# Overlapping pipelines for the chunks of a delta rule, an output projection by tiles, and a last product and norm in pieces

## The chip, the core and the metric

The kernel runs on one core of a Trainium2 chip. The metric is the time of one execution on the device, in microseconds (us). The engines of the core work side by side, each through its own list of instructions in a fixed order, and wait for each other through semaphores: TensorE (PE) multiplies matrices into PSUM, of which the kernel uses eight banks of 128 x 512 float32; VectorE (DVE), ScalarE (ACT) and GpSimd (POOL) work on tiles; SyncE (SP) issues most transfers. Weight loads of PE have a column of their own (PEld). Times come from executions of the whole program; the profile and the trace come from one profiled execution.

## The reference

A transformer-like layer of width 1024 on 1024 tokens: a feed-forward block, a mixer and a second feed-forward block, each with a residual and a norm ahead, and a last norm.

```python
h = h + 0.5 * swiglu_ffn(rmsnorm(h, ffn1_norm), ffn1_w_in, ffn1_w_out)
u = rmsnorm(h, mix_norm) @ w_mix_in
cb, cc, ch, gq, gk, gv, gz, gb, ga = split(u)
y_conv = short_conv_mixer(cb, cc, ch, conv_short_w, conv_out_norm)
y_gdn = gated_deltanet_mixer(gq, gk, gv, gz, gb, ga, ...)
h = h + concatenate([y_conv, y_gdn]) @ w_mix_out
h = h + 0.5 * swiglu_ffn(rmsnorm(h, ffn2_norm), ffn2_w_in, ffn2_w_out)
return rmsnorm(h, final_norm)
```

The delta rule has 4 heads of 128 and goes over the tokens in chunks. The part that matters here is, for each chunk (decay from the running sum g of the gates):

```python
lower = strict(k_beta @ k.T * decay)
u, w = solve_unit_lower(lower, [v_beta, k_beta * exp(g)])
attn = causal(q @ k.T * decay)
v_new = u - w @ state
o = (q * exp(g)) @ state + attn @ v_new
state = state * exp(g_last) + (k * exp(g_last - g)).T @ v_new
```

The kernel takes chunks of 128 tokens, so there are eight.

## The kernel before

Activations lie with channels on partitions and tokens along the free axis, in two halves of 512 tokens. Every wide product is done in split float32: each operand is cut into a rounded part hi and a rest lo (`split`, L102 on ACT and L103 on DVE), and `mm3` issues three matmuls of 128 x 128 by 512, hi by hi, lo by hi and hi by lo (L191 to L193). Such a group is called a triple here. `mm3` ends in `tick()`, which counts triples; `later(n, f)` has f emitted n triples on.

The stages: products of the first feed-forward block (0 to about 686 us), the norm and the q, k, v projection (to about 838), the delta rule with the z and convolution projections (to 1151), the output projection (to 1241 and, in its last part, beyond), the second feed-forward block (to 1939) and the last norm.

Within the feed-forward blocks and the output projection, work comes as a list of tasks with three parts: loads, preparation (sums of weights on POOL, splits on ACT and DVE) and the run of triples. `run_tasks` emits a task's loads up to nine tasks and its preparation up to four tasks ahead of its run. `ffn_out` does its product as seven block products of eleven steps each (L539 on); each step has four triples, one for each of four banks, and an `add` behind a product adds the four banks into the residual (L554). After the fifth product half 0 of the residual is complete; its norm runs beside products six and seven: squares on ACT (L209), their sum on POOL or DVE (L211), `after(n, m)`, which has the sum over channels taken by PE (L225) n triples later and the factor spread by PE (L243) m triples after that.

In the delta-rule stage PE has two sources of work. The z and convolution units (`rest`, 16 units of 16 triples = 256) are independent of the chunks and cover them: `pump(n)` emits n triples of them. The chunk work comes from generators, a `yield` between steps:
- `build(c)`, five steps, one chunk: loads q, k, v; transposes k, q, v on PE (`flip`, L868); the decay matrix `dec` and `eb` from products with a mask (L950, L974) and exponentials on ACT; `kd` (L954, on DVE, read from the PSUM bank of the k transpose); K times K (L862) into `lt`, Q times K into `at`; all results go to DRAM.
- `solve(g)`, 33 steps: inverts the 32 x 32 diagonal blocks of four chunks on DVE (L1030, L1034).
- `finish(c)` and `scan(c)`: load a chunk's results, complete the inverse on PE, and carry the state from chunk to chunk; the chunk's output `ot` is scaled on ACT (L1149), flipped and written.
- `late_convs`: the convolutions of the second half of q, k, v (L774), one in two steps.

`drive` runs one main generator step, then `pump`, then some steps of a side generator. Chunk follows chunk: builds 0 to 3 with the late convolutions beside them, builds 4 to 7 with `solve(0)`, inverse and scan of chunks 0 to 3 with `solve(1)`; those of chunks 4 to 7 run between tasks of the output projection (`mix_out`). Small products use four PSUM banks in turn (tag `aux`), wide ones the four others (`mm`); a bank is free for the next product when its last reader is done. A scheduler behind the program may move instructions within what the dependences allow; from then on each engine's order is fixed.

## Time and profile before

| what | value |
|---|---|
| time, median of 3 runs | 1960.46 us (1956.25 to 1960.53) |
| profiled execution, time | 1959.77 us |
| profiled execution, span from first to last instruction | 1958.0 us |
| mean clock granted to PE | 0.971 |
| instructions | 25016 |
| DMA | 312.45 MB, mean 160 GB/s |

How to read it: the span is shorter than the time by what lies before the first and behind the last instruction. An engine's share of busy time is a mean over all stages; the stages are seen in the row of 40 equal slices, in which each digit is the busy share in tenths (PEclk: the granted clock in tenths):

```profile
PE   5799999999999899987799989998999999999996
DVE  4876666567865797776974356688666566677655
PEclk9899999999999999998999979998999999999998
```

A slice is 49 us. The dip in the row of PE at slices 18 and 19 (from 0) is the beginning of the delta-rule stage; the last slice holds the last norm.

### The profile page before, as it was taken

The numbers are of one execution on the slowest core, as the hardware profiler recorded it, in microseconds if no ns is written. First come the engines' busy times: TensorE is split into PE (matmuls) and PEld (weight loads), VectorE is DVE, ScalarE is ACT, GpSimd is POOL, SyncE is SP. The second block draws the span as 40 slices with busy tenths as digits, with TensorE's granted clock in tenths as the row PEclk, the third lists the DMA queues.
The fourth block names the chain that finished last, engine by engine and source line by source line (L and its number), as shares of the span: only waits on it lengthen the run. The fifth ranks groups of instructions, "written<-read, shape, count | busy, mean of one in ns | idle before, by whom it ended". The sixth has DMA issues, their size and how long they took to land.

```text
span 1958.0 us, 25016 instructions
## 1 busy us (share of the span) xinstructions
PE 1833.8 (94%) x8512; PEld 1493.6 (76%) x8512; DVE 1338.5 (68%) x1991; ACT 750.0 (38%) x1517; POOL 733.3 (37%) x510
## 2 busy tenths in 40 slices
PE   5799999999999899987799989998999999999996
PEld 4578888888888777676678877776888888888884
DVE  4876666567865797776974356688666566677655
ACT  6422323223544453377332243452323222344433
POOL 1464455355331434145311001036454355435142
PEclk9899999999999999998999979998999999999998
DMA  7144343437883423477742176423343434487532
GB/s 281 33 161 128 118 140 127 140 108 257 311 270 113 140 97 102 141 245 252 222 135 80 61 263 183 164 92 102 127 139 127 140 109 160 150 292 274 193 108 97
DMA packets 194512, 312.45 MB, mean 160 GB/s; under 512 B 27856, under 2 KB 48336, under 8 KB 194384
## 3 DMA queue, kind: packets, MB, share of 16 engines
q1 hardware_dynamic: 191216, 305.28, 47.0%
q10 hardware_dynamic: 3168, 5.57, 0.9%
q8 instruction: 67, 1.10, 0.2%
q14 instruction: 61, 0.50, 0.1%
HBM read 228.44 MB, written 82.33 MB: 159 GB/s over the span
## 4 chain that ended last, share of the span: by engine, by line
PE 74%; DVE 13%; issue 4%; DMA 3%; POOL 3%; ACT 3%; SPq 0%; POOLq 0%; DVEq 0%; ACTq 0%
PE ps_ps L192 20%; PE ps_ps L191 20%; PE ps_ps L193 20%; PE ps_mm L191 3%; PE ps_mm L192 3%; PE ps_mm L193 3%; DVE wlo L103 3%; PE ps_aux L862 1%; DVE lo L103 1%; DVE xb L1034 1%; DVE sv L1030 1%; DVE cv L774 1%; POOL T L110 1%; DMA raw<-w_in 1%; DVE h L301 1%
## 5 line engine op out<-in xcount | busy, mean ns | idle before, releaser
L191 PE MATMUL ps_ps<-hi,whi 128*128 128x512 f32 x1400 | 554.1, 396 | 23.0 <-DVE c L389 11.4
L193 PE MATMUL ps_ps<-hi,wlo 128*128 128x512 f32 x1400 | 552.7, 395 | 13.0 <-DVE wlo L103 12.9
L192 PE MATMUL ps_ps<-lo,whi 128*128 128x512 f32 x1400 | 553.0, 395 | 5.3 <-DVE lo L103 5.2
L103 DVE TENSOR_TENSOR wlo<-raw,whi 128x512 fp32r<-128x512 f32 x280 | 267.3, 964 | 119.4 <-ACT whi L102 118.4
L103 DVE TENSOR_TENSOR wlo<-T,whi 128x512 fp32r<-128x512 f32 x244 | 235.3, 978 | 144.5 <-ACT whi L102 142.4
L191 PEld LDWEIGHTS ps_ps<-hi,whi 128*128 128x128 f32 x1400 | 266.8, 191 | 85.4 <-issue 12.3
L193 PEld LDWEIGHTS ps_ps<-hi,wlo 128*128 128x128 f32 x1400 | 267.3, 191 | 71.7 <-DVE wlo L103 16.0
L192 PEld LDWEIGHTS ps_ps<-lo,whi 128*128 128x128 f32 x1400 | 266.9, 191 | 63.1 <-DVE lo L103 8.0
L110 POOL TENSOR_TENSOR T<-raw 128x512 f32<-128x512 f32 x144 | 224.6, 1561 | 232.3 <-DMA raw<-w_out 91.5
L191 PE MATMUL ps_ps<-ghi,whi 128*128 128x512 f32 x616 | 241.8, 393 | 7.2 <-ACT whi L102 7.2
L192 PE MATMUL ps_ps<-glo,whi 128*128 128x512 f32 x616 | 241.9, 393 | 1.4 <-DVE glo L103 1.4
L193 PE MATMUL ps_ps<-ghi,wlo 128*128 128x512 f32 x616 | 241.7, 393 | 1.2 <-DVE wlo L103 1.2
L102 ACT CAST whi<-raw 128x512 fp32r<-128x512 f32 x280 | 170.2, 617 | 86.1 <-PE ps_mm L192 19.1
L102 ACT CAST whi<-T 128x512 fp32r<-128x512 f32 x244 | 146.4, 617 | 81.4 <-POOL T L110 44.8
L191 PE MATMUL ps_mm<-hi,whi 128*128 128x512 f32 x384 | 158.0, 412 | 0.9 <-DVE u L400 0.9
L192 PE MATMUL ps_mm<-lo,whi 128*128 128x512 f32 x384 | 155.2, 404 | 1.2 <-DVE lo L103 1.2
L193 PE MATMUL ps_mm<-hi,wlo 128*128 128x512 f32 x384 | 154.2, 402 | 1.4 <-DVE wlo L103 1.4
L103 DVE TENSOR_TENSOR glo<-raw,ghi 128x512 fp32r<-128x512 f32 x154 | 128.9, 838 | 38.8 <-ACT ghi L102 37.2
L191 PEld LDWEIGHTS ps_ps<-ghi,whi 128*128 128x128 f32 x616 | 116.3, 189 | 33.6 <-ACT whi L102 8.4
L193 PEld LDWEIGHTS ps_ps<-ghi,wlo 128*128 128x128 f32 x616 | 116.3, 189 | 28.0 <-DVE wlo L103 2.7
L192 PEld LDWEIGHTS ps_ps<-glo,whi 128*128 128x128 f32 x616 | 116.4, 189 | 27.3 <-DVE glo L103 2.1
L110 POOL TENSOR_TENSOR T<-raw,T 128x512 f32<-128x512 f32 x50 | 73.3, 1465 | 167.2 <-DMA raw<-w_in 129.3
(226 smaller groups left out, 2286.5 us busy)
## 6 DMA issues: line engine op xcount, KB each, us to landing
raw<-w_in SPq DMA_DIRECT2D x264, 256.0 KB, 4.6
raw<-w_out SPq DMA_DIRECT2D x154, 256.0 KB, 4.3
raw<-w_qkv SPq DMA_DIRECT2D x36, 256.0 KB, 3.4
f1S<-S SPq DMA_DIRECT2D x33, 256.0 KB, 5.0
raw<-f1A SPq DMA_DIRECT2D x33, 256.0 KB, 3.9
raw<-f1S SPq DMA_DIRECT2D x33, 256.0 KB, 3.7
f2S<-S SPq DMA_DIRECT2D x33, 256.0 KB, 5.0
raw<-f2A SPq DMA_DIRECT2D x33, 256.0 KB, 4.5
```

Source lines behind the costliest of these rows:

```text
L102: tc.keep_in_program_order(nc.scalar.copy(out=hi, in_=src))
L103: nc.vector.tensor_tensor(out=lo, in0=src, in1=hi.bitcast(F32), op=ALU.subtract)
L110: tc.keep_in_program_order(nc.gpsimd.tensor_tensor(out=out, in0=in0, in1=in1, op=op))
L191: nc.tensor.matmul(out=ps, lhsT=whi, rhs=xhi, start=start, stop=False, skip_group_check=True)
L192: nc.tensor.matmul(out=ps, lhsT=whi, rhs=xlo, start=False, stop=False, skip_group_check=True)
L193: nc.tensor.matmul(out=ps, lhsT=wlo, rhs=xhi, start=False, stop=stop, skip_group_check=True)
L301: nc.vector.tensor_tensor(out=s2, in0=s2, in1=s1, op=ALU.subtract)
L774: nc.vector.scalar_tensor_tensor(out=acc, in0=u[:, i:i + HALF], scalar=vcol(wc + i), in1=acc, op0=ALU.mult, op1=ALU.add)
L862: nc.tensor.matmul(out=ps[:, sl], lhsT=lhs[:, sl], rhs=rhs[:, sl], start=start, stop=stop)
L1030: nc.vector.tensor_tensor(out=tv, in0=lrow[:, lo:hi].unsqueeze(2).broadcast_to([nb, n, j + 1]), in1=xrow[:, 0:j + 1].unsqueeze(1).broadcas ...
L1034: nc.vector.tensor_tensor(out=xv, in0=xv, in1=tv, op=ALU.subtract)
```

## The change

1. `pipeline(gens, lag)` steps several generators in turn; the next one starts when the last one has gone `lag` steps. Builds 0 to 5 go through it with lag 3 (the late convolutions and then `solve(0)` beside them), builds 6 and 7 and then `solve(1)` become the side work of the inverses and scans of chunks 0 to 3, which go through it with lag 5; those of chunks 4 to 7 too, beside the output projection.
2. In `build`, a step boundary is put behind the first loads, and the mask product for `eb` stands ahead of `kd`. In `scan`, a step boundary is put ahead of the flip of `ot`.
3. One set of 22 tiles (`gd`) serves the builds and then the scans, cut in two ways by `rings`, so that several builds have tiles of their own.
4. `PACE`, the triples of cover per step, goes from 2.5 and 4.5 to 3.0 and 2.6.
5. `mix_out` has a task for each of eight output tiles instead of four tasks of two tiles.
6. The norm beside products six and seven starts 14 triples after the fifth instead of 26 (first block) and 30 (second block).
7. In the second block, the last four steps of product seven are done tile by tile, each tile's add right behind it.
8. The last norm is done in two halves of columns, with 16 output transfers instead of 8 for half 1, and ACT applies its share of the gain ahead of the spread.

```diff
-PACE = (2.5, 4.5)
+PACE = (3.0, 2.6)
...
+            def one(d, stop):
+                x, w = ops["x"], ops["w"]
+                ds = slice(d * P, (d + 1) * P)
+                mm3(banks[d], w[0][:, ds], w[1][:, ds], x[0], x[1], start and k == 0, stop)
+
+            if held is None:
+                task(run, ready, loads)
+            else:
+                held.append(one)
+                task(None, ready, loads)
...
-            task(add)
+            if not by_tile:
+                task(add)
+                return
+            for d in range(KH):
+                task(lambda d=d: [one(d, i == KH - 1) for i, one in enumerate(held)] and add([d]))
...
-            nm[0].after(26, 4)
+            nm[0].after(14, 4)
...
+        gd_tiles = [slot(F32, "gd") for _ in range(22)]
+        ring, used = {"r0": [slot(F32R, "r0") for _ in range(2)]}, {}
+
+        def rings(**counts):
+            n = 0
+            for name, b in counts.items():
+                ring[name] = gd_tiles[n:n + b]
+                n += b
...
                 r0.append(r)
+            yield
...
             pd = psum("aux")
...
+            pe = psum("aux")
+            for i, r in enumerate(r0):
+                nc.tensor.matmul(out=pe, lhsT=mask[:, P:2 * P], rhs=r, start=(i == 0), stop=(i == 1))
             dec = gt_tile("dec")
             nc.scalar.activation(out=dec, in_=pd, func=AF.Exp)
+            eb = gt_tile("eb")
+            nc.scalar.activation(out=eb, in_=pe, func=AF.Exp)
...
             yield
+            yield
             pyt = flip(ot)
...
+        def pipeline(gens, lag):
+
+            gens, live = list(gens), []
+            while gens or live:
+                if gens and (not live or live[-1][1] >= lag):
+                    live.append([gens.pop(0), 0])
+                for e in list(live):
+                    if next(e[0], live) is live:
+                        live.remove(e)
+                    else:
+                        e[1] += 1
+                        yield
...
+        def second_half():
+            for _ in pipeline([build(c) for c in (6, 7)], 6):
+                pump(PACE[1])
+                yield
+            solving = solve(1)
+            for _ in solving:
+                next(solving, None)
+                yield
+
+        rings(qT=3, kT=3, vT=3, v=2, dec=3, kd=2, lt=2, eb=2)
+        drive(pipeline([build(c) for c in range(CPH)], 3), PACE[0], late, 1)
...
+        drive(pipeline([build(c) for c in (4, 5)], 3), PACE[0], side, 3)
...
+        side = second_half()
+        drive(pipeline([inverse_and_scan(c) for c in range(CPH)], 5), PACE[1], side, 1)
...
             for u in range(4):
-                task(lambda u=u: run(u), lambda u=u: ready(u), lambda u=u: loads(u))
+                task(lambda u=u: run(u, 0), lambda u=u: ready(u), lambda u=u: loads(u))
+                task(lambda u=u: run(u, 1))
...
         def between():
-            for _ in range(4):
+            for _ in range(2):
                 next(scans, None)
...
-            last[0].after(30, 4)
+            last[0].after(14, 4)
...
+        for i in range(2):
+            for b in range(2 * i, 2 * i + 2):
+                nc.tensor.matmul(out=last[1].rb[:, b * P:(b + 1) * P], lhsT=rs[:, b:b + 1].broadcast_to([P, P]),
+                                 rhs=ident, start=True, stop=True)
+            scale_out(1, slice(2 * i * P, (2 * i + 2) * P))
```

The change moves instructions on every engine. At three places the built order of before and of the change stand here.

PE, from the k flip of build 2 to that of build 3 and K times K, before. `kT`, `qT` and `vT` are a chunk's k, q and v; `ps_aux` and `ps_mm` with a number are the uses of the small and the wide banks; L974 is the mask product for `eb`, L950 that for `dec`:

```order
L862 MATMUL ps_aux_7815<-kT_7305 128x128 x4
L974 MATMUL ps_aux_7849<-r0_7314,mask_7331 128x512
L974 MATMUL ps_aux_7849<-r0_7315,mask_7331 128x512
L862 MATMUL ps_aux_7854<-qT_7303,kT_7305 128x128 x4
L868 MATMUL ps_aux_7871<-cs_68,qT_7303 128x128 x4
L868 MATMUL ps_aux_7913<-cs_68,vT_7307 128x128 x4
L868 MATMUL ps_aux_7934<-cs_68,kT_7306 128x128 x4
L950 MATMUL ps_aux_7950<-r0_7314,mask_7331 128x512
L950 MATMUL ps_aux_7950<-r0_7315,mask_7331 128x512
L862 MATMUL ps_aux_7968<-kT_7306 128x128 x4
```

The change on PE, a k flip (of `gd_7307`) and what follows it; L968 and L971 are now the mask products for `dec` and `eb`, L885 the flip, and `gd_7309` is a v tile of another chunk:

```order
L885 MATMUL ps_aux_7595<-cs_68,gd_7307 128x128 x4
L968 MATMUL ps_aux_7611<-r0_7325,mask_7331 128x512
L968 MATMUL ps_aux_7611<-r0_7326,mask_7331 128x512
L971 MATMUL ps_aux_7614<-r0_7325,mask_7331 128x512
L971 MATMUL ps_aux_7614<-r0_7326,mask_7331 128x512
L885 MATMUL ps_aux_7633<-cs_68,gd_7309 128x128 x4
L191 MATMUL ps_mm_7580<-hi_5611,whi_7411 128x512
L192 MATMUL ps_mm_7580<-lo_5612,whi_7411 128x512
L193 MATMUL ps_mm_7580<-hi_5611,wlo_7412 128x512
L191 MATMUL ps_mm_7580<-hi_5616,whi_7411 128x512
```

Before, the steps of two builds stand one behind the other, with no wide matmul between them. Now a step of a build is followed by wide matmuls; after the last row shown come ten more of them, and then K times K of `gd_7307`, so fourteen wide ones lie between this chunk's flip and its K times K.

SP, where the output projection starts, before. `y_dr001` is the second piece of the convolution's output for half 0 of the tokens, `y_dr011` that for half 1; the loads of `raw` from `y_dr000` and `y_dr001` are the first operands of the projection, and L1046 and L1049 load results of a chunk:

```order
L1184 DMA y_dr001_7262<-acc_9936 128x512
L1049 DMA xc_10761<-diag_x1_7397 128x4x32
L1155 DMA y_dr100_7265<-zt_7325 256x1x128
L1155 DMA y_dr101_7266<-zt_7325 256x1x128
L1046 DMA lts_7324<-st_lt5_7381 128x512
L1184 DMA y_dr011_7264<-acc_10009 128x512
L95 DMA raw_10249<-y_dr000_7261 128x512
L95 DMA raw_10251<-y_dr000_7261 128x512
L95 DMA raw_10253<-y_dr001_7262 128x512
```

The change at the same place, where L1064 and L1067 are the loads of a chunk and L1203 the write of the convolution's output:

```order
L1153 DMA gd_7323<-z_dr1_7260 128x4x128
L1067 DMA xc_10620<-diag_x1_7397 128x4x32
L1064 DMA gd_7322<-st_lt5_7381 128x512
L1203 DMA y_dr001_7262<-acc_9987 128x512
L95 DMA raw_10240<-y_dr000_7261 128x512
L95 DMA raw_10242<-y_dr000_7261 128x512
L95 DMA raw_10244<-y_dr001_7262 128x512
L95 DMA raw_10246<-y_dr001_7262 128x512
```

The first loads of the projection stood behind the write of `y_dr011`; they now stand directly behind that of `y_dr001`, and the write of `y_dr011` follows seventeen places later.

DVE at the end of the program, before. L554 adds a bank into the residual `h`, L211 sums the squares into `nacc`, L217 makes the mean, L1387 scales an output tile:

```order
L554 SCALAR_TENSOR_TENSOR h_15741<-ps_ps_17075,h_15741 128x512
L211 TENSOR_TENSOR nacc_17043<-nacc_17043,sq_17268 128x512
L554 SCALAR_TENSOR_TENSOR h_15771<-ps_ps_17076,h_15771 128x512
L211 TENSOR_TENSOR nacc_17043<-nacc_17043,sq_17272 128x512
L211 TENSOR_TENSOR nacc_17043<-nacc_17043,sq_17276 128x512
L211 TENSOR_TENSOR nacc_17043<-nacc_17043,sq_17280 128x512
L217 TENSOR_SCALAR ms_17288<-ps_ps_17283 128x4
L1387 SCALAR_TENSOR_TENSOR h_15677<-h_15677,vs_66,ps_ps_17292 128x512
```

The change at the same place, where L563 adds, L1456 makes the mean of two of the four token blocks, and L1430 scales half of an output tile:

```order
L563 SCALAR_TENSOR_TENSOR h_15741<-ps_ps_17077,h_15741 128x512
L211 TENSOR_TENSOR nacc_17043<-nacc_17043,sq_17267 128x512
L563 SCALAR_TENSOR_TENSOR h_15771<-ps_ps_17078,h_15771 128x512
L211 TENSOR_TENSOR nacc_17043<-nacc_17043,sq_17283 128x512
L1456 TENSOR_SCALAR last_ms_17288<-ps_ps_17287 128x2 x2
L1430 SCALAR_TENSOR_TENSOR h_15677<-h_15677,vs_66,ps_ps_17286 128x256
L1430 SCALAR_TENSOR_TENSOR h_15741<-h_15741,vs_66,ps_ps_17286 128x256
```

The sums of squares no longer stand in a row behind the adds: each follows its own add, and the ten scalings of half tiles take the place of five of whole tiles.

More of the change, by code (lines that the diff above doesn't have):

```diff
@@ L493, in early_heads, with ffn_out @@
             task(*p.head2())
-    def ffn_out(acc, fill, g_dr, w_out, t1_done, t2_done):
+    def ffn_out(acc, fill, g_dr, w_out, t1_done, t2_done, by_tile=False):
         tsum = {}
@@ L503, in get, with step @@
             return load(w_out[2 * k + row][:, c * HALF:(c + 1) * HALF])
-        def step(banks, a, b, k, start):
+        def step(banks, a, b, k, start, held=None):
             r, ops = {}, {}
@@ L537, in run, with product @@
                 for d in range(KH):
-                    ds = slice(d * P, (d + 1) * P)
-                    mm3(banks[d], w[0][:, ds], w[1][:, ds], x[0], x[1], start and k == 0, k == NK - 1)
-            task(run, ready, loads)
-        def product(banks, a, b, start, *to, then=None, after=None):
+                    one(d, k == NK - 1)
+            def one(d, stop):
[7 more added lines that the diff above has]
+                task(None, ready, loads)
+        def product(banks, a, b, start, *to, then=None, after=None, by_tile=False):
+            held = []
             for k in range(NK):
-                step(banks, a, b, k, start)
+                step(banks, a, b, k, start, held if by_tile and k >= NK - KH else None)
                 if KH <= k < KT:
@@ L548, in product, with add @@
                         task(lambda tile_=tile_: fill(*tile_))
-            def add():
-                for d in range(KH):
+            def add(ds=range(KH)):
+                for d in ds:
                     for n in to:
@@ L970, in build @@
             yield
-            pe = psum("aux")
-            for i, r in enumerate(r0):
-                nc.tensor.matmul(out=pe, lhsT=mask[:, P:2 * P], rhs=r, start=(i == 0), stop=(i == 1))
-            eb = gt_tile("eb")
-            nc.scalar.activation(out=eb, in_=pe, func=AF.Exp)
-            nc.vector.tensor_copy(out=cols(per_chunk["gl"], c), in_=heads(eb)[:, :, C - 1])
             pq = psum("aux")
@@ L1276, in drive @@
                     next(side, None)
-        def inverse_and_scan(c):
-            yield from finish(c)
-            yield from scan(c)
-        for c in range(CPH):
-            drive(build(c), late, PACE[0], 2)
+        def second_half():
[8 more added lines that the diff above has]
+        drive(pipeline([build(c) for c in range(CPH)], 3), PACE[0], late, 1)
         for _ in late:
@@ L1286, in tile_hybrid @@
         side = solve(0)
[L1287 to L1288 removed]
+        drive(pipeline([build(c) for c in (4, 5)], 3), PACE[0], side, 3)
         for _ in side:
             pass
[L1291 to L1293 removed]
+        rings(qT=2, kT=1, vT=1, v=1, dec=1, kd=1, lt=1, eb=1, kg=2, qg=2, vs=2, kds=2, at=2, lts=1, zt=1, ot=1)
+        side = second_half()
+        drive(pipeline([inverse_and_scan(c) for c in range(CPH)], 5), PACE[1], side, 1)
         for _ in side:
@@ L1393, in out_t1, with out_t2 @@
                 last[0].square(d)
-            last[0].after(30, 4)
-            last[0].then(lambda: scale_out(0))
-        ffn_out(acc, fill, g_dr, w2_out, out_t1, lambda d: last[1].square(d, nc.vector))
-        run_tasks()
-        last[1].reduce()
-        last[1].spread()
-        scale_out(1)
+            last[0].after(14, 4)
+            last[0].then(lambda: [gain(0, d) for d in range(KT) if pre_scaled(d)] and scale_out(0))
+        def out_t2(d):
+            last[1].square(d, nc.vector)
+            if pre_scaled(d):
+                gain(1, d)
+        ffn_out(acc, fill, g_dr, w2_out, out_t1, out_t2, by_tile=True)
+        run_tasks()
+        last[1].rb = psum()
+        sums = psum()
+        ms, rs = (const.tile([P, 4], F32, name=n) for n in ("last_ms", "last_rs"))
+        for i in range(2):
+            two = slice(2 * i, 2 * i + 2)
+            for b in range(2 * i, 2 * i + 2):
+                nc.tensor.matmul(out=sums[:, b:b + 1], lhsT=last[1].acc[:, b * P:(b + 1) * P], rhs=ones[:, 0:1],
+                                 start=True, stop=True)
+            nc.vector.tensor_scalar(out=ms[:, two], in0=sums[:, two], scalar1=1.0 / D, scalar2=EPS,
+                                    op0=ALU.mult, op1=ALU.add)
+            nc.gpsimd.tensor_tensor(out=rs[:, two], in0=ms[:, two], in1=pneg[:, two], op=ALU.pow)
+        for i in range(2):
+            for b in range(2 * i, 2 * i + 2):
+                nc.tensor.matmul(out=last[1].rb[:, b * P:(b + 1) * P], lhsT=rs[:, b:b + 1].broadcast_to([P, P]),
+                                 rhs=ident, start=True, stop=True)
+            scale_out(1, slice(2 * i * P, (2 * i + 2) * P))
         while queue:
```

79 lines of the change are left out of this document (36 added, 43 removed).

## The prediction

> **What bounds the kernel now.** I read the page first: busy time by engine, and the chain of work that ended last.
>
> ```profile
> PE 1833.8 (94%) x8512; PEld 1493.6 (76%) x8512; DVE 1338.5 (68%) x1991; ACT 750.0 (38%) x1517; POOL 733.3 (37%) x510
> PE 74%; DVE 13%; issue 4%; DMA 3%; POOL 3%; ACT 3%; SPq 0%; POOLq 0%; DVEq 0%; ACTq 0%
> ```
>
> TensorE (PE) is busy 94% of the span and is 74% of the chain. The change takes no matrix product away, so it can only win time in which PE stands still or runs at a low clock. The next view cuts the stages that the change rewrites into windows. Columns: window, length, then busy us and instructions of PE, weight loads, VectorE (DVE), ScalarE (ACT) and GpSimd (POOL), the clock granted to PE, the DMA share, GB/s.
>
> ```profile
> core 0: us, PE busy (x) PEld busy (x) DVE busy (x) ACT busy (x) POOL busy (x), PEclk, DMA share, GB/s
> 838.00:907.00 69.00, 54.91 (x258) 44.46 (x257) 48.72 (x92) 54.36 (x132) 31.05 (x24) 0.85 0.80 262
> 907.00:988.00 81.00, 66.52 (x340) 54.74 (x338) 62.85 (x182) 34.39 (x114) 30.17 (x25) 0.94 0.69 213
> 988.00:1123.00 135.00, 132.91 (x844) 108.12 (x844) 72.76 (x201) 38.23 (x103) 12.83 (x9) 1.00 0.30 91
> 1123.00:1151.00 28.00, 21.80 (x157) 19.42 (x156) 12.52 (x30) 10.32 (x30) 2.60 (x2) 0.70 0.56 180
> 1151.00:1241.00 90.00, 84.75 (x546) 67.47 (x545) 52.96 (x106) 34.42 (x93) 14.39 (x12) 0.94 0.65 209
> 890.00:900.00 10.00, 6.40 (x21) 4.82 (x22) 8.15 (x16) 9.80 (x25) 5.91 (x4) 0.50 0.78 267
> ...
> 1440.00:1480.00 40.00, 40.00 (x178) 33.12 (x178) 26.01 (x32) 10.90 (x20) 18.14 (x12) 1.00 0.37 126
> ```
>
> The windows are: builds 0 to 3 (838 to 907), builds 4 to 7 (907 to 988), the first four scans with the second solve (988 to 1123), the passage to the output projection (1123 to 1151), and that projection with the last scans (1151 to 1241). The last row is a stage with no gap, for comparison: 40.00 / 178 = 0.225 us for one wide matmul.
>
> What each window loses, I count as idle time plus (1 - clock) times busy time. Builds 0 to 3: 69 - 54.91 = 14.1, and 0.15 x 54.91 = 8.2, so 22.3 us. Builds 4 to 7: 14.5 + 0.06 x 66.52 = 18.5. First scans: 2.1. Passage: 6.2 + 0.30 x 21.80 = 12.7. Projection: 5.3 + 0.06 x 84.75 = 10.3. That is **66 us** in 403; more than these cannot come from this part of the program. Each fast stretch needs its neighbours to be fast, as the row of 890 to 900 shows: PE is busy 6.4 of 10 us, and runs at half clock besides.
>
> **The change part by part.**
>
> *Builds.* A build turns one chunk's q, k, v into what the scans need. The groups of PE show where it stands still; after the second bar is the idle time before a group, and what ended it.
>
> ```profile
> L868 PE MATMUL ps_aux<-cs,ot 128*128 128x128 f32 x32 | 9.8, 357 | 6.8 <-ACT ot L1149 6.8
> ...
> L868 PE MATMUL ps_aux<-cs,vT 128*128 128x128 f32 x32 | 5.9, 314 | 11.4 <-DVE kd L954 6.6 <-ACT eb L976 2.7 <-issue 2.1
> ...
> L868 PE MATMUL ps_aux<-cs,kT 128*128 128x128 f32 x32 | 5.7, 305 | 8.9 <-DVE cv L774 4.3 <-DMA kT<-qkv_dr 2.3 <-DVE xb L1034 1.4
> L868 PE MATMUL ps_aux<-cs,qT 128*128 128x128 f32 x32 | 5.4, 294 | 2.0 <-DVE bk L945 1.9
> ```
>
> Of the 28.6 us idle in the two build windows, 22.3 stand before the three flips (transposes) of the builds. The v flip waits 11.4 in all, mostly for kd: the four auxiliary PSUM banks go round, and the v flip takes the bank that kd is read from. In the order of before, sixteen small matmuls and no wide one lie between the two flips at the place shown. In the new order, steps of two builds alternate with wide triples, so these 11.4 and the q flip's 1.9 are what I expect to go: **13.3**.
>
> A wait takes their place. In the new order, the mask product for eb is issued earlier, so the K-times-K product now takes kd's bank. How long kd takes today, from the k flip on PE to kd on DVE:
>
> ```profile
> 914.67 0.63 PE L868 MATMUL ps_aux<-cs,kT 128*128 128x128 f32 x4 [0.66 <-ACT whi L102]
> ```
> ```profile
> 921.67 0.67 DVE L954 TENSOR_TENSOR kd<-ps_aux,dec 128x512 f32<-128x512 f32 x1
> ```
>
> That is 922.34 - 914.67 = 7.7 us to kd's end. Between the k flip and the K-times-K product the new order has fourteen wide matmuls in the place shown (14 x 0.225 = 3.1 us), the flip itself and another (0.6 each) and four mask products, together about 5 us. Today's 7.7 includes work of DVE that stood before kd only because two late convolution or three solve steps ran per build step. Bounds for the new wait: 0, and 8 builds x (7.7 - 5) = 22. I take 1 us each, **8**, since the squares and the exponential of the same chain are all that remains. Queued behind K-times-K on PE are the triples themselves, so all of it is lost time.
>
> The k flip's 8.9 is for DVE (4.3 for cv, a late convolution; 1.4 for the solve) and for its load (2.3). The late convolutions run one step per build step instead of two, though more steps overlap; their work is the same. I take half of cv and load as gone, **3.3**. Clock: 8.2 + 4.0 = 12.2 us are lost to it; with the gaps about halved I take half, **6.1**. Builds: 13.3 - 8 + 3.3 + 6.1 = 14.7, rounded to **14.5** (bounds: 13.3 - 22 = -8.7, and all of 40.8).
>
> The Trainium skill, "TensorE: Matmul & The Clock Gate", Part 1 (The HAM clock gate), says that the clock is either half or full, that half follows an idle window of about 3.4 us, and that a busy window of that length brings full back. The 0.50 of 890 to 900 agrees with the half; no row here shows the window's length. By this rule gaps that all fall under that length would bring back all 12.2 us and the sum would be 6 us lower.
>
> *First scans.* Two builds and the second solve move into this window, and two scans overlap. It loses 2.1 us now, so it can hardly gain; cover per step falls from 4.5 triples to 2.6, but there are more steps. I take **0** (bounds: +2, and a loss as dense as that of builds 4 to 7, 2 builds x 18.5 / 4 = 9). The same 256 triples of z and convolution are spread, none added.
>
> *Passage and output projection.* SyncE's (SP's) queue, in order:
>
> ```profile
> 1129.95 0.32 SPq L1184 DMA_DIRECT2D y_dr<-acc  x1
> ...
> 1139.76 0.35 SPq L1184 DMA_DIRECT2D y_dr<-acc  x1
> 1140.15 2.12 SPq L95 DMA_DIRECT2D raw<-y_dr  x4
> 1142.37 8.80 SPq L95 DMA_DIRECT2D raw<-w_mo  x8
> ```
>
> The projection starts with half 0 of the convolution output, the last quarter of which is written at 1129.95. Its loads stand behind the write of half 1 (1139.76) and go at 1140.15: 10.2 us later, with PE at a clock of 0.70. In the new order these loads stand right behind the half-0 write, ahead of the half-1 write. I take the 10.2 us as saved up to what the window loses, 12.7: **10** (bounds 0, if the eight weight loads of 8.80 us set the start, and 12.7). A second term: in the projection the scans' flip of ot waits 6.8 us for ACT; the extra step before it and the second scan beside it put wide triples there. I take all, **6.8** (bounds 0 and 10.3). Together **17**.
>
> *Norm in the first feed-forward output.* Waits of PE between 640 and 700, and POOL's queue there:
>
> ```profile
> PE ps_ps L191 <- ACT whi L102: 3.1, 2, 2.2
> ...
> PE ps_ps L193 <- DVE wlo L103: 1.2, 2, 0.8
> ```
> ```profile
> 660.19 4.06 POOL L211 TENSOR_TENSOR nacc<-nacc,sq 128x512 f32<-128x512 f32 x3 [16.01 <-ACT sq L209]
> 664.21 4.64 POOL L110 TENSOR_TENSOR nT<-nT,raw 128x512 f32<-128x512 f32 x3
> ```
>
> PE loses 4.3 us as product 7's weights stand on POOL behind the sums of squares, which come late since DVE did the norm's multiplications right before. With the norm 12 triples (12 x 0.675 = 8 us) earlier, that work meets product 6 instead, whose operands are prepared four tasks ahead. I take **4** (bounds 0, as preparations for product 6 now fall behind the norm, and 5).
>
> *Norm and last product in the second feed-forward output.*
>
> ```profile
> PE ps_ps L191 <- ACT whi L102: 4.1, 1, 4.1
> ...
> PE ps_ps L192 <- DVE glo L103: 0.6, 1, 0.6
> ```
> ```profile
> 1903.12 3.70 SPq L1389 DMA_DIRECT2D out_dram<-h  x6
> ```
> ```profile
> 1912.66 4.47 POOL L110 TENSOR_TENSOR nT<-nT,raw 128x512 f32<-128x512 f32 x3 [4.89 <-DMA raw<-w_out]
> ```
>
> Six output writes stand in SP's queue ahead of the last weights, POOL waits 4.89 us for these, and PE then 4.7. In the new order the norm comes 16 triples (11 us) earlier, and the writes stand three steps further from the end. Against it: the last four steps of the last product are now taken tile by tile, so its first tile needs the operands of the last step 3 steps (9 triples beyond the first tile's own three, 6 us) sooner. I take **4.5** (bounds 0 and 4.7 plus 1.7 for the clock).
>
> *Tail.*
>
> ```profile
> 1938.94 0.39 PE L193 MATMUL ps_ps<-ghi,wlo 128*128 128x512 f32 x1
> ...
> 1942.83 1.87 PE L225 MATMUL ps_ps<-cs,nacc 128*128 128x1 f32 x8 [3.49 <-DVE nacc L211]
> ...
> 1948.78 3.38 DVE L1387 SCALAR_TENSOR_TENSOR h<-h,vs,ps_ps 128x512 f32<-128x512 f32 x5 [3.88 <-ACT rbs L1380]
> ...
> 1950.12 3.98 ACTq L1389 DMA_DIRECT2D out_dram<-h  x4
> ```
>
> By tile, only one add, square and sum follow the last matmul instead of DVE's heap: of 3.49 us I take 1.2 as saved. The norm in two halves saves little: in the built order the second half's spread on PE waits for DVE's last multiplication of the first half, as both lie in one PSUM tile, and ScalarE's copy stands behind its output issues, so the pieces come one after the other. The last output issues on ACT (1950.12 to 1954.10) are fewer and smaller: about 1.3. Sum **2.5** (bounds 0, as twice the instructions may cost twice the fixed time, and 4).
>
> The Trainium skill, "PSUM — Partial Sum Buffer", section "PSUM bank collisions raise a hardware error", says that two engines must be kept from one bank at the same time, whatever the columns. The row of 1948.78 agrees in part: DVE reads the spread only after ACT's copy of it. By this rule no order of these pieces in one bank overlaps; with two banks the sum would have about 2 us more.
>
> **Sum.** 14.5 + 0 + 17 + 4 + 4.5 + 2.5 = 42.5 us. The profiled execution took 1959.77 (span 1958.0 and 1.8 around it), 0.7 under the median of 1960.46; 1959.77 - 42.5 = 1917.3, so **1917**.
>
> **Rivals.**
>
> *The other engines bind in the builds.* DVE is busy 48.72 + 62.85 of 150 us there and ACT 54.36 of the first 69; 9.80 of 10 in the row of 890. Late convolutions, solve steps and builds are the same work on them. For it: between 838 and 907 ACT leaves just 14.6 us. Against it: over both windows ACT has 88.75 of 150. Then builds gain nothing, and the first scans with two builds lose up to 9: 1917 + 14.5 = 1932, up to 1941. 25%.
>
> *Nearly everything goes.* Pipelines hide the new wait too and the clock stays full: 66 - 31.5 = 34 more, less what an edge between stages must cost, say a quarter of 66: about 1900, at the very best 1883. 13%.
>
> *Slower: the bank ring of builds.* With two builds live and four auxiliary banks, every product of a build, not K-times-K alone, waits for a reader of the other build, PE being in order. If three of the five steps wait the 2.7 us (7.7 - 5), this is 8 x 3 x 2.7 = 65 instead of the 8 I took: 1917 + 57 = 1974. It decides from (42.5 + 6) / 8 = 6 us per build over my value. For it: the wait on kd is in the built order. Against it: the other readers (exponential, lt, at) are single operations of 0.6 to 1.4 us. 6%.
>
> *The change doesn't do it:* loads of the projection stay bound by the eight weight loads and the norms by DVE. Then 17 and 8.5 fall away: 1942. 8%.
>
> **How the numbers follow.** My forecast (1905 to 1926) has 44%, the others as given; the remaining 4% are mixtures near no change. What a measurement here can tell from no change is 0.3%, 5.9 us (1954 to 1966). Faster: 44 + 25 + 13 + 8 = 90%, less 2 for the tails of the last two: 88%. Within 0.3%: 5%. Slower: 7%. The range 1890 to 1946 takes in the first rival's upper end, the fourth rival and most of the best case; outside are the slower rival, no change and the best of the best, 17%.
>
> **What would show it.** Right: PE's clock at 0.95 or more in the build stage; the wait of the v flip for kd gone; loads of y directly behind the half-0 write and the first output product some 18 us after the last convolution triple or sooner; no wait of 4 us for weights in the last product; the time from the last wide matmul to the end 2 to 3 us shorter than 1958.0 - 1939.3 = 18.7. Wrong: DVE or ACT busy over 95% of the builds; K-times-K waiting over 3 us per build; a new gap where builds 6 and 7 lie among the first scans.

## The result and the profile after

The changed kernel took 1905.0 us (median of 4 runs, 1902.51 to 1906.43), the kernel before 1958.36 beside it (4 runs, 1952.78 to 1960.53). The ratio is 0.9726 (95% interval 0.9703 to 0.9749), so it is faster by 2.7%. The profiled execution took 1906.43, its span is 1904.4: 53.6 us shorter than the span before. The forecast was 1917 with 1890 to 1946.

The page of the changed kernel, busy time by engine:

```profile
PE 1816.6 (95%) x8512; PEld 1483.8 (78%) x8512; DVE 1337.0 (70%) x1997; ACT 747.3 (39%) x1518; POOL 732.2 (38%) x514
```

PE has the same 8512 matmuls; every engine does the same work in a shorter span. Windows of the changed kernel follow (columns as before); the first three rows are builds 0 to 3, builds 4 and 5 with the rest of the first solve, and the scans with builds 6, 7 and the second solve. Then come the passage to the output projection, and the projection.

```profile
830.00:899.00 69.00, 62.97 (x316) 50.19 (x315) 53.15 (x94) 55.95 (x137) 32.15 (x25) 0.98 0.82 269
899.00:958.00 59.00, 51.47 (x243) 42.78 (x243) 46.32 (x132) 20.99 (x63) 19.25 (x15) 0.88 0.74 234
958.00:1100.00 142.00, 140.20 (x930) 115.73 (x930) 90.44 (x261) 50.84 (x163) 23.83 (x19) 1.00 0.40 124
1100.00:1118.00 18.00, 16.32 (x151) 14.68 (x148) 9.37 (x22) 5.94 (x15) 1.63 (x1) 0.62 0.69 207
1118.00:1198.00 80.00, 78.55 (x511) 65.52 (x512) 51.78 (x103) 33.55 (x94) 14.25 (x12) 1.00 0.65 218
```

Counted as in the prediction, the losses are 6.0 + 1.3 = 7.3, 7.5 + 6.2 = 13.7, 1.8, 1.7 + 6.2 = 7.9 and 1.5 us: 32 in place of 66. Builds lose 21 instead of 40.8, although two of them now lie in the scans, which lose no more than before; the passage 7.9 instead of 12.7; the projection 1.5 instead of 10.3.

Where in the program the 53.6 us came from is read on PE: the start of the n-th triple in both traces, and the difference (from the 1461st on the order of the triples is alike again).

```
triple    before     after   ahead by
 851       628.7     628.7      0.0     before product 7 of the first block
 951       708.0     702.0      6.0
1101       835.3     827.3      8.0     first builds
1461      1268.6    1228.7     39.9     second feed-forward block begins
1651      1417.4    1374.0     43.4
2351      1897.8    1854.4     43.4     last product
2400      1938.5    1888.3     50.2     last triple
end       1958.0    1904.4     53.6
```

At product 7, with the norm beside it, the change gains 6.0 us, from the first builds to the second block 31.9, in the last product 6.8 and in the tail 3.4. The 2.0 us between triples 951 and 1101 and the 3.5 between 1461 and 1651 are not credited to the change: the kernels below that have it, with the early norm, take 125.3 to 127.6 and 143.5 to 148.1 us there, the kernel before 127.3 and 148.8. The triples between 1651 and 2351, which the change leaves alone, take the same time to 0.1 us.

The flips of the builds and of `ot`, which had 29.1 us of idle time ahead of them in four rows, are one row now (L885), with K times K and its like in L879, and no wait for `kd`:

```profile
L879 PE MATMUL ps_aux<-gd 128*128 128x128 f32 x184 | 26.9, 293 | 1.8 <-ACT gd L973 0.8 <-DVE gd L1021 0.8
L885 PE MATMUL ps_aux<-cs,gd 128*128 128x128 f32 x128 | 21.1, 284 | 8.4 <-DMA gd<-qkv_dr 4.1 <-ACT junk L1008 1.7 <-DVE gd L999 1.1
```

SP's queue at the passage: the loads now stand right behind the half-0 write, as the order showed, but the first output product starts at 1118.69, 13.6 us after them (11.1 before).

```profile
1104.40 0.32 SPq L1203 DMA_DIRECT2D y_dr<-acc  x1
1105.07 2.22 SPq L95 DMA_DIRECT2D raw<-y_dr  x4
1107.34 8.70 SPq L95 DMA_DIRECT2D raw<-w_mo  x8
```

Tail:

```profile
1891.31 0.61 PE L1454 MATMUL ps_ps<-cs,nacc 128*128 128x1 f32 x4 [2.17 <-DVE nacc L211]
...
1896.82 1.19 PE L1461 MATMUL ps_ps<-cs,last_rs 128*128 128x128 f32 x4 [2.63 <-POOL h L1428]
...
1898.49 2.09 POOL L1428 TENSOR_TENSOR h<-h,rbs 128x256 f32<-128x256 f32 x3 [1.74 <-ACT rbs L1424]
1899.25 1.70 ACTq L1432 DMA_DIRECT2D out_dram<-h  x3
```

The second spread waits 2.63 us for the first half's scaling: the halves come one after the other.

### The profile page after: what moved, and what is told of

Its sections match the earlier page's. It is cut to its first block, busy times and chain, and to the rows that moved or that the text cites. A ratio compares the mean times of both kernels' runs of the same rounds, so it can differ in the third digit from the quotient of the medians.

```text
span 1904.4 us, 25000 instructions
## 1 busy us (share of the span) xinstructions
PE 1816.6 (95%) x8512; PEld 1483.8 (78%) x8512; DVE 1337.0 (70%) x1997; ACT 747.3 (39%) x1518; POOL 732.2 (38%) x514
## 4 chain that ended last, share of the span: by engine, by line
PE 44%; DVE 4%; issue 1%; DMA 1%; ACT 1%; POOL 1%; SPq 0%; POOLq 0%; DVEq 0%; ACTq 0%
PE ps_ps L191 10%; PE ps_ps L193 10%; PE ps_ps L192 10%; PE ps_mm L191 3%; PE ps_mm L193 3%; PE ps_mm L192 3%; DVE wlo L103 1%; PE ps_aux L879 1%; DVE lo L103 1%; PE ps_aux L921 0%; PE ps_aux L1147 0%; PE ps_mm L1199 0%; PE ps_aux L1146 0%; PE ps_mm L1185 0%; PE ps_aux L885 0%
## 5 line engine op out<-in xcount | busy, mean ns | idle before, releaser
L103 DVE TENSOR_TENSOR wlo<-T,whi 128x512 fp32r<-128x512 f32 x244 | 239.3, 994 | 145.3 <-ACT whi L102 144.0
L103 DVE TENSOR_TENSOR wlo<-raw,whi 128x512 fp32r<-128x512 f32 x280 | 261.6, 952 | 101.6 <-ACT whi L102 98.5
L191 PEld LDWEIGHTS ps_ps<-hi,whi 128*128 128x128 f32 x1400 | 265.6, 190 | 84.0 <-issue 10.2
```

The costliest lines, as they stand in the source:

```text
L103: nc.vector.tensor_tensor(out=lo, in0=src, in1=hi.bitcast(F32), op=ALU.subtract)
L191: nc.tensor.matmul(out=ps, lhsT=whi, rhs=xhi, start=start, stop=False, skip_group_check=True)
```

## The experiments

Each is the changed kernel with one edit, three rounds beside the kernel before. One measure from each trace helps where the times are too close: the stage, from the 1101st to the 1461st triple on PE (the same work in all); the passage, from the last convolution triple to the first output triple; and the longest stretch without a wide matmul in the builds (825 to 1000 us), with the small matmuls in it.

```
kernel               median us   ratio to before          stage  passage  longest stretch
before               -           1                        433.3   28.5    22.6 us, 46 small
changed              1905.0      0.9726 (0.9703-0.9749)   401.4   19.7     7.6 us, 16
builds apart         1906.5      0.9741 (0.9720-0.9762)   402.5   14.5     6.2 us, 16
apart, few tiles     1906.0      0.9739 (0.9714-0.9763)   402.4   21.4     6.2 us, 16
scans apart          1916.4      0.9793 (0.9773-0.9813)   405.9   19.1     6.9 us, 8
eb late              1909.1      0.9757 (0.9738-0.9776)   402.1   19.6     8.8 us, 16
old pace             1918.8      0.9801 (0.9778-0.9824)   409.0   27.0    16.1 us, 104
twelve ticks         1907.4      0.9738 (0.9716-0.9759)   396.7   19.9     7.3 us, 16
weights early        1904.9      0.9722 (0.9700-0.9745)   394.6   10.9     6.6 us, 8
norms late           1921.1      0.9804 (0.9783-0.9824)   401.0   19.8     7.0 us, 16
three banks          1907.0      0.9732 (0.9710-0.9753)   401.6   15.2     5.2 us, 8
late two             1905.7      0.9740 (0.9714-0.9765)   401.5   14.5     7.6 us, 8
builds first         1910.1      0.9759 (0.9728-0.9791)   405.5   19.8     9.4 us, 16
no step              1907.6      0.9743 (0.9722-0.9763)   398.3   14.5     6.4 us, 12
```

Only three intervals lie clear of the changed kernel's: scans apart, old pace and norms late. The column of the stage is one execution each: kernels whose times cannot be told apart lie between 394.6 and 405.5 us in it. No run undoes the tasks by single output tiles, the last steps tile by tile or the last norm in halves; what is said of these is read from the traces.

The passage needs a warning. In the changed kernel and in seven of the others (builds apart, apart with few tiles, eb late, norms late, late two, builds first, no step) PE runs the same 155 matmuls in the same order there, and waits 2.4 to 2.7 us in all. In the changed kernel the clock falls to half within the passage, and it takes 19.7 us. With builds apart the clock stays full, and it takes 14.5; so it does with late two and with no step:

```profile
1100.30:1114.80 14.50, 11.86 (x156) 10.31 (x154) 9.49 (x23) 6.73 (x17) 1.64 (x1) 1.00 0.61 185
```

The waits of PE in the passage of the changed kernel (1099 to 1119):

```profile
PE ps_mm L191 <- ACT whi L102: 1.0, 1, 1.0
PE ps_aux L879 <- DVE gd L1122: 0.8, 1, 0.8
PE ps_aux L921 <- DVE pm L1084: 0.6, 1, 0.6
```

So what fills it is the small products of the scans, and the clock they get; the first output product waits 1.0 us for its split weights. A difference of 5 us in this column says nothing of an edit. A steadier measure is the time from the last convolution triple to the second block: 129.7 us in the changed kernel, 127.2 to 131.5 in all others but old pace (149.0), scans apart (135.3) and weights early (123.2), and 145.9 before.

**Builds one after the other.**

```diff
-        drive(pipeline([build(c) for c in range(CPH)], 3), PACE[0], late, 1)
+        drive(pipeline([build(c) for c in range(CPH)], 99), PACE[0], late, 1)
-        drive(pipeline([build(c) for c in (4, 5)], 3), PACE[0], side, 3)
+        drive(pipeline([build(c) for c in (4, 5)], 99), PACE[0], side, 3)
```

> The changed kernel, but builds 0 to 3 and 4, 5 run one after the other (a lag of 99 instead of 3). Theory of the overlap: the build stage loses about 20 us of PE time less than before because two builds alternate with wide triples (loss of idle and clock 40.8 us before, about 21 after); one after the other again, most of it returns: 1905 + 15 to 20 = 1920 to 1925, and the v flip waits for kd again (6 us or more in all flips beyond the 8.4 of the changed kernel). Rival, the cover: it is the larger number of triples per build step (3.0 instead of 2.5, six steps instead of five) that fills the gaps; then the time stays within 5 us of 1905.

1906.5 us, stage 402.5 against 401.4: the theory of the overlap falls for builds 0 to 5. No flip waits for `kd` without the overlap either. This is the change's headline, and in this place it is worth nothing that can be measured. Builds 6 and 7 have a lag of 6, as many as a build has steps, so they do not overlap in the changed kernel either.

**Scans one after the other** (the same edit, 5 to 99, in both pipelines of `inverse_and_scan`).

> The changed kernel, but inverses and scans run one chunk after the other, both beside the second solve and beside the output projection (a lag of 99 instead of 5). Theory of the overlap: the projection's loss fell from 10.3 to about 1.5 us because the flip of ot no longer waits (6.8 us before), for which the second scan's steps stand in between; apart again, 5 to 9 us return: 1910 to 1914. Rival: the extra step ahead of the flip and the smaller tasks are what removed the wait; then the time is within 3 us of 1905. A third: the scans apart finish later than the projection and leave a tail of small products without cover, 1920 or more.

1916.4, some 11 us slower by the medians. The trace has 4.5 of it in the stage (5.6 by the steadier measure); in the projection the flip waits for `ot` (scaled by ACT in L1167) again. Rows of PE's flips, 1098 to 1206 with the scans apart:

```profile
L885 PE MATMUL ps_aux<-cs,gd 128*128 128x128 f32 x16 | 4.3, 310 | 4.0 <-ACT gd L1167 4.0
```

and 1098 to 1200 in the changed kernel:

```profile
L885 PE MATMUL ps_aux<-cs,gd 128*128 128x128 f32 x16 | 3.0, 293 | 0.2 <-ACT gd L1167 0.2
```

Another 3.8 us of this trace lie in the last product (37.7 us against 33.9; others of these kernels take 33.7 to 36.0), which the edit does not touch. The overlap of scans is real, some 11 us by the times, of which this one trace places about 5.

**eb late** (the mask product, exponential and copy stand ahead of Q times K again).

> The changed kernel, but the mask product, the exponential and the copy for eb stand ahead of Q times K again, as before. The prediction's theory: with eb early, K times K takes the bank that kd is read from and waits for it (I took 8 us in all; the trace of the changed kernel shows under 2); without it the time is 2 to 8 us shorter, 1897 to 1903. Rival: eb early is what took the table load and the exponential of eb out of the path of the v flip (2.7 us waited for eb before), so the time is 3 to 10 us longer, 1908 to 1915. If neither, within 2 us of 1905: the place of eb does not matter once builds overlap.

1909.1, with an interval that overlaps; stage 402.1 against 401.4. The prediction's theory falls, as nothing gets shorter. The time lies in the range of the rival, 4 us longer, but the stage, where it would show, is the same; that the place of `eb` matters is not shown.

**Old pace** (`PACE = (2.5, 4.5)`).

> The changed kernel with the old numbers of covering triples per step, 2.5 and 4.5 instead of 3.0 and 2.6. Theory of the overlap: the 256 covering triples are only spread differently; with 4.5 per step in the stage of the first scans they run out before the eight scans' steps there are done, and the last of these stand without cover: 1905 + 5 to 15. Rival: the numbers hardly matter, within 3 us of 1905. Rival, the cover: the gain of the build stage was due to 3.0, so the build stage alone grows by over 10 us.

1918.8: 14 us slower by the medians, 6.3 in the profiled execution, the fastest of its four. The trace shows the theory's place: the last convolution triple comes at 1086.4 us instead of 1099.0, so the cover is gone before the scans of the first half are, and the window from 958 to 1100 loses 8.0 + 1.3 us instead of 1.8:

```profile
958.00:1100.00 142.00, 134.01 (x872) 111.30 (x872) 84.50 (x233) 48.34 (x147) 23.47 (x18) 0.99 0.35 107
```

The passage takes 27.0 us. The builds did not lose more, so the rival of the cover falls as far as 15 triples a build (six steps of 2.5) go: the stretch of 104 small matmuls is where scans already run (from 956.8).

**Twelve ticks** (twelve counts ahead of the projection; both writes ahead of its loads again).

> The changed kernel with twelve counts and four scan steps ahead of the output projection instead of four counts and four steps; in the built order both writes of the convolution's output then stand ahead of the projection's first loads again. The prediction's theory: the loads go some 5 to 10 us later, as before, and the first product with them: 1910 to 1915. Rival: the eight weight loads behind them (8.7 us of issue) and the small products of the overlapping scans set the start anyhow; within 2 us of 1905.

1907.4, passage 19.9 against 19.7. The loads do go later, at 1109.21, behind both writes (1103.22 and 1108.84), where they went 0.7 us behind the first; PE has more small products ahead of the projection here (179 matmuls in the passage). The time does not tell the two places apart, so which write the loads stand behind is worth nothing that can be measured.

**Weights early.**

```diff
+        order += [w_mo[0, u] for u in range(2)]
         loaded, ahead = [], []
...
+                if (part, hf) == (0, 0) and u < 2:
+                    return
                 w[u] = [load(w_mo[part, u][:, i * HALF:(i + 1) * HALF]) for i in range(2)]
...
+                if (part, hf) == (0, 0) and u < 2:
+                    w[u] = ahead.pop(0) if u == 0 else [wsplit(r) for r in loaded.pop(0)]
```

> The changed kernel, and the first two of the projection's weight tiles of each column pair are loaded (and the first is split) with the units of the convolution projection, well ahead of the convolution's output. Theory: in the changed kernel the passage from the last convolution triple (1099.7 us) to the first output product (1118.7 us) still loses about 8 us, as the first product waits for weights that are issued behind the convolution's output; with these there early, the first product comes 3 to 6 us sooner: 1899 to 1902. Rival: the convolution's output itself (its load and its split) comes last, or the small products of the scans fill the time on PE anyhow: within 2 us of 1905.

The passage falls to 10.9 us and the stage by 6.8. But the built order has only 115 matmuls in the passage now instead of 155, and the clock is full:

```profile
1100.00:1110.80 10.80, 9.12 (x117) 7.73 (x115) 6.19 (x16) 4.24 (x11) 1.63 (x1) 1.00 0.55 161
```

The first output product, which waited 1.0 us for its weights, no longer does; in the projection PE then waits 4.1 us for split weights, where the changed kernel waits 3.9 with that 1.0. So waits for weights did not go away: from the last convolution triple to the second block PE waits 6.7 us in all here and 6.9 in the changed kernel, while the time lost to half clock (half of its length) is 1.7 us instead of 10.2. The shorter time of this trace is that of the clock. The time is 1904.9, not told apart from 1905.0, though the profiled execution (1901.25) is shorter; the other runs of this kernel reach 1907.25, so that it is a better kernel isn't shown.

**Norms late** (26 and 30 triples instead of 14).

> The changed kernel with the norms beside products six and seven 26 (first block) and 30 (second block) triples after the fifth product, as before. The prediction's theory: the first block loses the 4 to 5 us of weight waits again, and the second the 4 to 7 us, as output writes stand ahead of the last weights: 1905 + 9 to 12 = 1914 to 1917. Rival for the second block: the order by tiles is what removed the wait of the last weights; then only the first block loses, 1909 to 1911.

1921.1: 16 us. The trace gives both parts. Product 7 of the first block takes 79.4 us as before (79.3), where every kernel with the early norm takes 72.7 to 73.4. The last product takes 41.8, where those take 33.7 to 37.7; there PE waits for weights once more and SP has six output writes at a late place:

```profile
PE ps_ps L191 <- ACT whi L102: 5.7, 1, 5.7
```
```profile
1867.42 3.65 SPq L1432 DMA_DIRECT2D out_dram<-h  x6
```

The order by tiles does not remove that wait; the rival falls.

**Three banks** (`"aux": 3`).

> The changed kernel with three auxiliary PSUM banks in turn instead of four. The slower rival of the prediction, the bank ring: products of PE wait in order for the reader of a bank; if the ring of four is near its limit with two builds live, a ring of three adds several us per build and per scan, over 30 us in all: 1935 or more. If four is ample, the waits grow by a few us: 1905 to 1915.

1907.0. In the builds (830 to 958) K times K waits 5.7 us where it waited 1.8, and the flips 3.4 where they waited 6.7:

```profile
L879 PE MATMUL ps_aux<-gd 128*128 128x128 f32 x96 | 13.2, 284 | 5.7 <-DVE gd L1021 4.4 <-ACT gd L975 1.2
L885 PE MATMUL ps_aux<-cs,gd 128*128 128x128 f32 x72 | 11.0, 275 | 3.4 <-DVE gd L987 1.3 <-DVE bk L963 1.3 <-DMA gd<-qkv_dr 0.7
```

The ring of four is not near its limit.

**Late convolutions two steps at a time** (`late, 2`).

> The changed kernel with two steps of the late convolutions per build step, as before, instead of one. With builds one after the other (an earlier run) and with three banks the time stayed, so the overlap of builds is not what emptied the build stage. Theory of the load: before, the late convolutions, two steps per build step, crowded ScalarE and VectorE during builds 0 to 2 (ScalarE busy 9.80 of 10 us at 890), and spreading them over all four builds is what helped; two per step bring back 6 to 14 us: 1911 to 1919. Rival: their rate does not matter either: within 3 us of 1905.

1905.7, stage 401.5. Their rate does not matter that can be measured.

**Builds 6 and 7 beside the first solve.**

```diff
-        drive(pipeline([build(c) for c in (4, 5)], 3), PACE[0], side, 3)
+        drive(pipeline([build(c) for c in (4, 5, 6, 7)], 3), PACE[0], side, 3)
...
-            for _ in pipeline([build(c) for c in (6, 7)], 6):
-                pump(PACE[1])
-                yield
```

> The changed kernel with builds 6 and 7 in one pipeline with 4 and 5, beside the first solve, instead of beside the first scans. Theory of the move: a build has too little cover in its own stage, and putting two of eight beneath the scans, which lost 2 us in 135, takes away a quarter of the loss of the builds (40.8 us before): 1905 + 8 to 12 = 1913 to 1917. Rival: the builds' loss is gone for other reasons (more cover per build, tiles of their own): within 3 us of 1905.

1910.1, stage 405.5, 4 us more; the intervals overlap. At most a small part.

**Few tiles, builds apart** (the first run's edit and `rings(qT=2, kT=2, vT=1, v=1, dec=2, kd=1, lt=1, eb=1)`).

> The changed kernel with builds 0 to 5 one after the other and the tiles per build as few as before (two for q, k and the decay, one for each of the others), where the run with builds one after the other had three and two. Theory of the tiles: with more tiles the loads of a build and its first steps need not wait until the last build's tiles are read or written out (k flips waited 2.3 us for loads, and 6.6 for kd, before): 1905 + 6 to 12 = 1911 to 1917. Rival: the tiles of before are enough where builds do not overlap: within 3 us of 1906.5, the time with builds one after the other.

1906.0, stage 402.4. With builds apart, the larger number of tiles is not what helps them.

**No step behind the loads** (the first `yield` of `build` out, `PACE = (3.6, 2.6)`).

> The changed kernel without the step boundary behind a build's first loads, and with 3.6 triples per build step instead of 3.0, so that a build of five steps has the same 18 triples. Theory of the step: the boundary puts triples between the loads of q, k, v and the k flip, and PE does not stand at the flip waiting for the load (4.1 us waited in the changed kernel, 8.9 at the k flips before): without it 4 to 10 us more, 1909 to 1915. Rival: the count of covering triples per build (12.5 before, 18 now) is what matters, not where they stand: within 3 us of 1905.

1907.6, stage 398.3. The step does not matter while the cover per build stays at 18 triples.

## Why the prediction was right, and where its steps were not

The time lies in the range, and the bound was read rightly: PE's losses in the rewritten places. That the sum comes near owes something to luck: the norms and the builds gave more than their terms, the passage less, and the reasons for the builds and the passage do not hold. Two of the signs named did not come either: PE's clock in the builds is 0.93 (830 to 958), not 0.95, and the first output product comes 19.7 us after the last convolution triple, not some 18. The terms, against what the traces show:

**Norms, 4 + 4.5: mis-sized.** They are worth about 6 in the first block and 4 to 8 in the last product by the traces, and 16 together by the times of the run that undoes them. The waits of the first block (4.3 us quoted, 5.0 with the third) fell to 0.8, a difference of 4.2, but PE got 6.0 us ahead there at a full clock: what stops PE costs more than the wait. For the last product I took 4.5 of 6.4; the run that undoes the norms shows 5.7 in a single wait, and a loss of clock behind it (3.4 us).

**Builds, 14.5: wrong in cause, so that the size is not far from the 19.8 measured is luck.** The step "with two builds live, their steps alternate with wide triples" failed as a reason: builds apart have the same time. So did the step "K times K takes kd's bank", 8 us: that row waits 1.8 in all, none of it for `kd`. (The three solve steps per build step, by which I explained the length of `kd`'s chain, are the changed kernel's; before there were two.) What went away is one stretch. Before, PE issued 46 small matmuls from 875.6 to 898.2 with no wide one among them; this is where the changed kernel gets 16.6 us ahead between two triples counted 25 apart (8.4 to 25.0). The windows 876 to 898 of the two kernels, first before, then after (the same times, not the same place in the program):

```profile
876.00:898.00 22.00, 10.90 (x45) 8.58 (x46) 14.22 (x28) 17.71 (x40) 9.67 (x7) 0.68 0.84 272
```
```profile
876.00:898.00 22.00, 19.71 (x93) 15.63 (x94) 17.49 (x36) 16.64 (x46) 7.36 (x7) 0.92 0.79 261
```

The next wide triple of before needed a weight tile that had been loaded from 860.06 on, and that ACT, busy 17.71 of 22 us with late convolutions and exponentials, split only at 896.08:

```profile
860.06 0.97 SPq L95 DMA_DIRECT2D raw<-w_z  x2
```
```profile
896.08 0.60 ACT L102 CAST whi<-raw 128x512 fp32r<-128x512 f32 x1
```

So in that place the cover itself was held up on ACT, in whose order the split stands behind that work, and PE had only the builds' small products. PE stood still for 11.1 of the 22 us, mostly for DVE and ACT (4.3 for `cv`, 2.7 for `eb`, 1.9 for `bk`), at a clock of 0.68. I had this as the first rival (the other engines bind), but put it down as a bound on the whole stage, which it is not: ACT has as much work in the first builds now (55.95 of 69 us). The stretch is absent from every variant that was run, whichever part was undone, so no single part of the change is needed for it. All of them give a build at least 15 triples of cover, where it was 12.5 before. Whether that is the reason, or several parts each suffice to break up this one place of the built order, **stays open**: adding only cover to the kernel of before was not tried, nor was only the rate of the solve steps put back.

**Passage and projection, 10 + 6.8: their sum not far off, the first step wrong.** The windows give 4.8 and 8.8. That the loads of y stood behind a write was not what set the start (twelve ticks: no change), and the weight loads behind them are not shown to set it either. I took PE to stand until the loads came. But before, in the 28.5 us of the passage, PE ran 159 matmuls and waited 6.3 us, all of it for other engines' part in the small products (2.8 for `rw`, a factor of the convolution's norm), none for loads or weights. These waits are 2.4 now, and the half clock lasts 13.7 us instead of 17.1. The wait for `ot` went as said, and with the scans' overlap, as the run with scans apart shows; the clock in the projection rose in this trace, from 0.94 to 1.00, which I had left out; with late two and no step as much of it is lost up to the second block as before (5.1 us), so this part is not shown to come from the change.

**First scans, 0: right**, 1.8 lost instead of 2.1. It hangs on the cover: with the old pace the scans run out of it.

**Tail, 2.5: near, 3.4.** By tile saves 1.3 us (the first sum waits 2.17 instead of 3.49), the two halves net 0.4 (they are serial, as I had said; the profile names POOL's last multiplication of the first half as what the second spread waits for, which ends 0.1 us after DVE's), the outputs behind the last result 1.7 (5.5 us from 1952.5 to the end before, 3.8 now).

The rival in which nearly everything goes did not come about: 32 of 66 us stay. The bank ring is refuted by the run with three banks. By the rule that the prediction quotes from the Trainium skill, "TensorE: Matmul & The Clock Gate", Part 1 (The HAM clock gate), half clock follows an idle window of about 3.4 us. In the builds of the changed kernel the trace leaves that open: there is one wait of 4.5 us and one of 3.1, and a clock of 0.88 from 899 to 958. In the passage it does not agree: the clock is at half from 1104.4 on, with PE busy 12.55 of 13.6 us, and in the 25 us ahead of it no wait of PE is over 0.6 us.

```profile
1079.00:1104.40 25.40, 24.32 (x177) 20.43 (x176) 10.38 (x26) 6.77 (x22) 2.64 (x2) 1.00 0.36 102
1104.40:1118.00 13.60, 12.55 (x88) 11.21 (x87) 5.84 (x13) 4.21 (x11) 1.63 (x1) 0.50 0.81 250
```

So here half clock came without such a window, in a run of small matmuls, and for the same matmuls it did not come in three other runs.

## What to carry to other kernels

Before crediting a new order with its idea, look for the one or two long stretches in which the bounding engine had no covering work, and ask which engine held the cover back; here one stretch was half of the gain of a stage, and the idea that was written in, overlapping builds, was none of it. Undo the parts one at a time: of ten parts undone, three had a measurable effect, and the simplest of them, starting a norm 12 to 16 triples earlier so that its output writes and sums are not ahead of the last weights, brought nearly a third. Before pricing what a transfer holds up, look whether the engine waits for it at all: PE had other work in the passage and did not. A wait that a new order makes possible should be priced with its cover, not at the chain's present length.

## What was not expected of the hardware

The same kernel's executions differ by 4 to 8 us (1902.51 to 1906.43 for the changed one, 1912.44 to 1920.60 with the old pace), so single profiles can stand 6 us from the median; a gain of 7 us seen in one trace (weights early) did not show in the times. A single stage can differ more than the whole: the same 155 matmuls with the same waits took 14.5 us at full clock and 19.7 where it fell to half for 13.7 us, and the projection behind them gave the difference back (129.7 us up to the second block in the changed kernel, 128.0 to 130.4 in the three at full clock). What decides between the two clocks is not shown. With three banks instead of four, K times K waited 3.9 us more in the builds, the flips 3.3 less, and the stage took the same time: the waits only changed their place.
